# A two-layer diffusion trunk on one core: layer 0's experts scatter four at a time per stream

## The chip, the cores and the metric

The kernel is one program on one core of a Trainium2 chip. It is measured in microseconds of device time, from several runs, of which the median counts. TensorE does the matrix products, VectorE, ScalarE and POOL (GpSimd) the rest, and SyncE issues nearly all DMA transfers.

## What is computed

A trunk of two layers works on two streams of 256 tokens with 1024 channels: the context (stream 0) and the latents (stream 1). Each layer mixes tokens by three branches (an S5 state-space scan, latent attention, window attention) and then applies a mixture of sixteen experts. Layer 0 does it for both streams, layer 1 for the latents alone. The part that matters here is the mixture:

```python
def expert_choice_ffn(h, lp):
    B, N, D = h.shape
    cap = CAPACITY_FACTOR * N // N_EXPERTS
    aff = jax.nn.softmax((h @ lp['w_router']).astype(jnp.float32), axis=-1)
    g, idx = lax.top_k(aff.swapaxes(1, 2), cap)
    xs = jax.vmap(lambda hb, ib: hb[ib])(h, idx)
    a = jnp.einsum('becd,edf->becf', xs, lp['w_gate'])
    u = jnp.einsum('becd,edf->becf', xs, lp['w_up'])
    y = jnp.einsum('becf,efd->becd', jax.nn.silu(a) * u, lp['w_down']) * g[..., None].astype(h.dtype)
    return jax.vmap(lambda ib, yb: jnp.zeros((N, D), yb.dtype).at[ib.reshape(-1)].add(yb.reshape(-1, D)))(idx, y)
```

Every expert picks its 32 best tokens of each stream, transforms them, weights them with the router's affinity and adds them back at the places of those tokens. The last line is the scatter.

## The kernel before

The network is written in Python with a framework that schedules: instructions are recorded in the order of the code, and a scheduler then sets the order in which they stand on each engine, by its own model of times. On each engine the order is fixed once the program is built; an instruction that waits holds up what stands behind it there.

**Weights.** `expert_ring` (L1391) is the stream of expert weights: tiles of 1 MB, twelve an expert (four each of gate, up and down), 192 a layer. Each tile has a buffer of 2048 columns, taken from a list `ready`; when TensorE has used up a tile its buffer goes back to the list and the next load is issued on SyncE's queue (`load`, L229). Every buffer carries the index of the load from which on it is no longer used for weights. In layer 0 some 21 buffers serve at first; five of them (the blocks big0 to big2) end with load 100, because layer 1's S5 set-up needs them, four with 160 and two with 172. Five are left at the end: the four halves of h0 and h1 and one piece of the arena.

**One expert.** `moe` (L1565) loops over the experts e. In layer 0 the two streams stand together: M = 64 rows (stream, slot), and the 1024 output columns are cut in CT = 2 pieces of NF = 512, which stand below each other on the 128 partitions of one PSUM tile. Gate and up products go to two PSUM tiles `sc`; ScalarE takes tanh (L1613), VectorE makes the gated product (L1614, L1615); four transposes (`tp`, L246) turn it and ScalarE copies it out (L238); the down product goes to a PSUM tile `mm`. All these products are recorded under L243, the helper `mm`. The tokens of experts 4g to 4g + 3 are collected by `gather` (L1544), again products into the PSUM tiles `F` and `ad`, after experts 0, 3, 6 and 8.

**The scatter.** VectorE weights the down product with the sixth modulation row and puts it into YS (L1635). YS has 128 rows and is filled by GE = 2 experts: (expert, stream, slot). Then a selection matrix is built for each of the four token tiles t (two per stream): the rows (expert, slot) of that stream are compared with the tokens' slots and multiplied by half the affinity (L1644, L1645), the rows of the other stream stay zero from a memset (L1631). It is transposed into a `tp` tile and copied into CM. Each tile t takes two products of 128x512 with CM as the weights and YS as the moving data, into `F` and `ad`, and VectorE adds each to the residual x[t] (L1659). After the last expert the products are accumulated in PSUM on top of x[t], brought in by a product with the identity, in the tiles `F`, `ad`, `sc`, `sc`, `tp`, `tp`, `mm`, `mm`. In short:

```python
if e % GE == GE - 1:
    scat = lambda pt, n, h, start: self.mm(pt, CM[:, n * 128:(n + 1) * 128], YS[:, halves[h]], start, True)
    for n, t in enumerate(tts):
        for h, hs in enumerate(halves):
            pt = self.ps(("F", "ad")[h])
            scat(pt, n, h, True)
            v.tensor_tensor(x[t][:, hs], x[t][:, hs], pt, op=OP.add)
```

**Beside it.** From expert 8 on `moe` also runs `s5_setup` (L507) for layer 1, three steps an expert. It begins with parameters of 48 KB (`in_s5_prm`), two powers on POOL (L549, L551), a chain of small VectorE operations (L546 and others), and then transposes on TensorE into `tp` tiles, in four rounds.

Of the kernel before, what the change touches and what calls it, by code (L numbers as in the profile page):

```python
# [9 lines left out]
AF = mybir.ActivationFunctionType  # L10
# [4 lines left out]
D = 1024  # L15
# [16 lines left out]
# ---------------------------------------------------------------- shape-only constants  # L32
# [125 lines left out]
class Net:  # L158
# [6 lines left out]
    # ------------------------------------------------------------ helpers  # L165
# [6 lines left out]
    def rot(self, name, cols, n, low=False, at=None):  # L172
        """n buffers used in turn: returns a function that gives the next one"""
# [21 lines left out]
    # ------------------------------------------------------------ work that fills the gaps of the tensor engine  # L195
# [3 lines left out]
    def tick(self, us):  # L199
        """issue about us of the work that waits in the queue"""  # L200
# [57 lines left out]
    def pow_(self, out, in_, e):  # L258
        """out = in_ ** e"""
# [19 lines left out]
    def ln_apply(self, out, x, eng="v"):  # L279
        """out = (x - mean) * rstd"""  # L280
# [13 lines left out]
    def ln_affine(self, P, x, y, gb, again=True, eng="v"):  # L294
        """x = LN(P) g + b, P: halves of the columns; y: scratch; gives minus mean and 1 / deviation of x"""
# [34 lines left out]
    def ln_final(self, out, x, nm, r2):  # L330
        """out = (x + nm) r2"""
# [6 lines left out]
    # ------------------------------------------------------------ adaLN parameters  # L338
# [12 lines left out]
    def ada_group(self, l, g, bufs=None):  # L351
        """columns 2048 g .. of the adaLN parameters: mods 2g and 2g + 1"""
# [33 lines left out]
    def mod_row(self, l, m, s, dst, scale=1.0):  # L386
        """dst [128, 1024] = mod m of stream s on every partition"""
# [17 lines left out]
    def put(self, dst, src):  # L405
        """src into the parts dst [rows, 2, n]"""
# [9 lines left out]
    def block(self, tag, dtype):  # L416
        """a block that serves one purpose after another"""
# [3 lines left out]
    def branch_parts(self, l, b, oT, q0):  # L421
        """both parts of a branch output, [128, 4, 512 - q0]"""
# [17 lines left out]
    def wsplit(self, st, a, n, scale=None):  # L440
        """weights st [128, a, n] (times scale [128, a, n]) in two parts: a function of row k (and columns)"""
# [37 lines left out]
        # two blocks (row block, stream) at a time; of the second layer first those of the context  # L479
# [26 lines left out]
    # ------------------------------------------------------------ S5: matrices from the parameters  # L506
    def s5_setup(self, l, S, NP):  # L507
        """matrices of the layer from its parameters, NP group pairs at a time"""
# [72 lines left out]
        # powers a^1 .. a^4 (r: real, imaginary, minus real, minus imaginary)  # L581
# [16 lines left out]
        # phase of a^4 in turns, in [-1/2, 1/2]  # L598
# [19 lines left out]
        for j0 in range(0, 16, NP):  # L618
# [7 lines left out]
            # bb = q b  # L626
# [9 lines left out]
            # a^k bb and c a^k, state-major  # L636
# [25 lines left out]
            # chunk input matrices: (s, h) of a group on partitions, states on columns  # L662
# [1278 lines left out]
```

## Time and profile before

| what | us |
|---|---|
| median of 3 runs | 2170.84 |
| lowest and highest run | 2166.41, 2172.0 |
| span of the profiled execution | 2167.7 |
| TensorE busy in it | 1856.2 (86%) |
| VectorE busy | 1041.5 (48%) |
| ScalarE busy | 613.4 (28%) |
| POOL busy | 454.4 (21%) |

The profiled execution is one execution of its own. Its span runs from the first to the last instruction; no other time of it is given, so the sum is made against the span, which lies 3.1 us below the median. Busy time on TensorE is modelled, since products overlap: a row of several products says when the first starts and how long all of them take together. "x8" behind a product in float32 counts records, of which one product leaves two. A row of the timeline gives start, length, engine, line, operation, output and input, count, and in brackets the idle time before it with what ended it. DMA share is the mean busy share of the core's 16 DMA engines; values just above 1 mean they never rested.

### The profile page before, as it was taken

The page shows a single profiled execution, that of the slowest core. Times are in us where ns is not written, and L with a number is a line of the kernel's source. Part 1 is how long each engine was busy: PE and PEld are TensorE (multiplying, and loading weights), DVE is VectorE, ACT ScalarE, POOL GpSimd, SP SyncE. Part 2 cuts the span into 40 slices and gives each one's busy share as a digit, 9 for nine tenths or more (in the row PEclk, how much of TensorE's full clock was granted, in tenths as well). Part 3 has the DMA queues.
Part 4 walks back from the last instruction along what each step waited for, and adds up shares of the span by engine and source line. Part 5 has one row for each costly group of instructions (what it writes and reads, how often), then busy time and mean ns, then how long its engine had stood idle before and what let it go on. Part 6 is the DMA issues. An engine that isn't in the chain of part 4 may idle for free. (4 is left out here: it accounts for less than half of the span.)

```text
span 2167.7 us, 31197 instructions
## 1 busy us (share of the span) xinstructions
PE 1856.2 (86%) x12121; PEld 1117.8 (52%) x12121; DVE 1041.5 (48%) x2463; ACT 613.4 (28%) x1353; POOL 454.4 (21%) x592
## 2 busy tenths in 40 slices
PE   5998999999998799999798979889998766666665
PEld 2876666666776434343333358777786533222222
DVE  7767666644538512222555165978767311010102
ACT  2344343433434311010111054654553100000000
POOL 5735420000135100000434033642114000000000
PEclk8999999999999899999899989899999787686766
DMA  7234533265347799989899823242267799999996
GB/s 304 65 127 142 159 131 111 72 206 185 92 133 285 273 382 409 409 350 378 329 375 355 324 76 96 74 142 79 75 221 249 303 409 409 409 409 409 409 409 271
DMA packets 222163, 544.16 MB, mean 251 GB/s; under 512 B 18624, under 2 KB 101696, under 8 KB 221120
## 3 DMA queue, kind: packets, MB, share of 16 engines
q1 hardware_dynamic: 222016, 542.18, 67.6%
q8 instruction: 95, 1.56, 0.3%
q14 instruction: 52, 0.43, 0.1%
HBM read 541.09 MB, written 1.05 MB: 250 GB/s over the span
## 5 line engine op out<-in xcount | busy, mean ns | idle before, releaser
L243 PE MATMUL F<-h,wc 128*128 128x256 f32 (+1 forms) x1200 | 239.5, 351 | 13.9 <-ACT arena L1291 9.7
L400 ACT ACTIVATE wc<-arena 128x512 fp32r<-128x512 f32 (+2 forms) x280 | 170.2, 619 | 229.3 <-DMA arena<-in_w_in 49.4
L403 DVE TENSOR_TENSOR wc<-arena,wc 128x512 fp32r<-128x512 f32 (+2 forms) x205 | 163.8, 809 | 121.7 <-ACT wc L400 120.7
L243 PE MATMUL sc<-arena,xs 128*32 128x256 f32 (+1 forms) x1176 | 171.8, 535 | 56.7 <-DMA arena<-in_w_up 36.3
L243 PEld LDWEIGHTS F<-h,wc 128*128 128x128 f32 x1200 | 189.6, 197 | 47.9 <-ACT arena L1291 10.8
L246 PE MATMUL tp<-const,arena 128*128 128x128 f32 (+2 forms) x835 | 137.6, 291 | 62.8 <-DVE arena L1615 13.4
L403 POOL TENSOR_TENSOR wc<-arena,wc 128x512 fp32r<-128x512 f32 (+2 forms) x75 | 99.3, 1324 | 431.1 <-ACT wc L400 305.9
L243 PE MATMUL mm<-arena 128*32 128x256 f32 (+5 forms) x1076 | 168.1, 460 | 16.4 <-DMA arena<-in_w_down 8.0
L246 PEld LDWEIGHTS tp<-const,arena 128*128 128x128 f32 (+2 forms) x835 | 98.4, 146 | 120.8 <-issue 34.8
L1635 DVE TENSOR_TENSOR arena<-mm,arena 32x256 f32<-32x256 f32 (+1 forms) x96 | 48.9, 510 | 220.5 <-PE mm L243 208.7
L238 ACT ACTIVATE arena<-tp 128x512 f32<-128x512 f32 (+3 forms) x142 | 63.1, 474 | 311.9 <-PE tp L246 311.4
L260 POOL TENSOR_TENSOR lnq<-lnq,k 128x1 f32<-128x1 f32 x22 | 16.4, 747 | 574.5 <-DVE lnq L307 538.3
L243 PEld LDWEIGHTS sc<-arena,xs 128*32 128x32 f32 (+1 forms) x1176 | 54.4, 134 | 152.0 <-issue 81.9
L243 PE MATMUL sc<-h,xs 128*32 128x256 f32 (+1 forms) x760 | 118.7, 529 | 15.6 <-DMA h<-in_w_up 8.2
L1613 ACT ACTIVATE arena<-sc 128x512 f32<-128x512 f32 (+1 forms) x32 | 15.7, 490 | 366.3 <-PE sc L243 364.0
L243 PEld LDWEIGHTS mm<-arena 128*64 128x64 f32 (+2 forms) x1076 | 69.6, 137 | 91.5 <-issue 44.5
L243 PE MATMUL sc<-big,xs 128*32 128x256 f32 (+1 forms) x688 | 95.0, 522 | 15.5 <-DMA big<-in_w_gate 8.9
L1615 DVE TENSOR_TENSOR arena<-arena,sc 128x512 f32<-128x512 f32 (+1 forms) x32 | 17.7, 553 | 176.1 <-PE sc L243 175.7
L243 PE MATMUL mm<-wc,h 128*128 128x512 f32 (+2 forms) x288 | 78.4, 397 | 11.0 <-ACT h L492 6.1
L243 PE MATMUL F<-extra,wc 128*128 128x256 f32 (+1 forms) x432 | 85.0, 342 | 2.7 <-DVE arena L1326 2.4
L546 DVE TENSOR_TENSOR arena<-arena 128x64 f32<-128x64 f32 (+2 forms) x300 | 81.5, 318 | 10.7 <-POOL arena L549 4.7
L243 PEld LDWEIGHTS sc<-h,xs 128*32 128x32 f32 (+1 forms) x760 | 36.5, 132 | 86.8 <-issue 49.8
(345 smaller groups left out, 3246.6 us busy)
## 6 DMA issues: line engine op xcount, KB each, us to landing
arena<-in_w_gate SPq DMA_DIRECT2D x53, 1024.0 KB, 11.3
arena<-in_w_down SPq DMA_DIRECT2D x48, 1024.0 KB, 12.5
arena<-in_w_up SPq DMA_DIRECT2D x44, 1024.0 KB, 18.2
arena<-in_w_ada SPq DMA_DIRECT2D x82, 512.0 KB, 4.6
h<-in_w_down SPq DMA_DIRECT2D x41, 1024.0 KB, 10.3
h<-in_w_up SPq DMA_DIRECT2D x37, 1024.0 KB, 10.5
arena<-in_w_in SPq DMA_DIRECT2D x66, 512.0 KB, 3.8
big<-in_w_gate SPq DMA_DIRECT2D x30, 1024.0 KB, 15.1
```

Of the source, the lines that this page charges most:

```text
L238: self.nc.scalar.activation(out, in_, AF.Copy)
L243: return self.nc.tensor.matmul(out, lhsT, rhs, start=start, stop=stop, skip_group_check=True)
L246: self.nc.tensor.transpose(out, in_, self.c("idn")[:n, :n])
L260: self.nc.gpsimd.tensor_tensor(out, in_, e.to_broadcast(list(in_.shape)), op=OP.pow)
L400: nc.scalar.activation(hi, src, AF.Copy)
L403: eng.tensor_tensor(lo, src, hi.bitcast(F32), op=OP.subtract)
L546: tt = lambda o, a, b, op: v.tensor_tensor(o, a, b, op=op)
L1613: nc.scalar.activation(th, gu[0][:, :NF], AF.Tanh, scale=0.5)
L1615: v.tensor_tensor(th, th, gu[1][:, :NF], op=OP.mult)
L1635: v.tensor_tensor(YS[o:o + M, c * NF:(c + 1) * NF], yp[M * c:M * c + M, :NF], m5[M * c:M * c + M], op=OP.mult)
```

## The change

In layer 0 four experts of one stream are scattered together. There are now two tiles YS, one per stream, each with the rows (expert, slot) of four experts, so that all 128 rows hold data; the weighted eviction writes 32 rows at a time. After every fourth expert the two streams follow one another: each builds the selection matrices of its own two token tiles, 128 rows without zeros, in one matrix `w` of 256 columns, transposes them, copies them into one CM of 256 columns, and does its four products. The memset goes. In layer 1, with one stream, the code does what it did. The place of CM in the arena moves. (The full diff also drops comments; those hunks are left out.)

```diff
-        GE = 128 // M
-        io = self.c("iota")[:, None, :].to_broadcast([128, GE, 32])
+        io = self.c("iota")[:, None, :].to_broadcast([128, 4, 32])
...
             if e == 0:
-                YS, w, CM = [self.buf(k, c, True, self.T[k]) for k, c in (("ys", D), ("rwt", NF), ("cm", NF))]
-                nc.gpsimd.memset(w, 0.0)
-                wv = w.rearrange("p (t e s c) -> p t e s c", t=nt, e=GE, s=NS)
-            o = (e % GE) * M
-            for c in range(CT):
-                v.tensor_tensor(YS[o:o + M, c * NF:(c + 1) * NF], yp[M * c:M * c + M, :NF],
-                                m5[M * c:M * c + M], op=OP.mult)
-            if e % GE == GE - 1:
-                g = e // GE
+                YS = [self.buf(f"ys{n}", D, True, self.T["ys"] + D * n) for n in range(NS)]
+                w, CM = [self.buf(k, 256, True, self.T[k]) for k in ("rwt", "cm")]
+                wv = w.rearrange("p (i e s) -> p i e s", i=2, e=4)
+            o = e % 4 * 32
+            for n in range(NS):
+                for c in range(CT):
+                    r = M * c + 32 * n
+                    v.tensor_tensor(YS[n][o:o + 32, c * NF:(c + 1) * NF], yp[r:r + 32, :NF], m5[r:r + 32], op=OP.mult)
+            if e % 4 == 3:
+                g = e // 4
...
-                for n, t in enumerate(tts):
-                    o = wv[:, n, :, n // 2]
-                    v.tensor_tensor(o, self.cd[t][:, es, None].to_broadcast([128, GE, 32]), io, op=OP.is_equal)
-                    v.tensor_tensor(o, o, self.ah[t][:, es, None].to_broadcast([128, GE, 32]), op=OP.mult)
-                    self.tr(tp[:, n * 128:(n + 1) * 128], wv[:, n].rearrange("p e s c -> p (e s c)"))
-                self.copy(CM, tp[:, :nt * 128], "a")
+                for n in range(NS):
+                    two = tts[2 * n:2 * n + 2]
+                    tp = self.ps("tp")
+                    for i, t in enumerate(two):
+                        v.tensor_tensor(wv[:, i], self.cd[t][:, es, None].to_broadcast([128, 4, 32]), io, op=OP.is_equal)
+                        v.tensor_tensor(wv[:, i], wv[:, i], self.ah[t][:, es, None].to_broadcast([128, 4, 32]), op=OP.mult)
+                        self.tr(tp[:, i * 128:(i + 1) * 128], wv[:, i].rearrange("p e s -> p (e s)"))
+                    self.copy(CM, tp[:, 0:256], "a")
+                    scat = lambda pt, i, h, start: self.mm(pt, CM[:, i * 128:(i + 1) * 128], YS[n][:, halves[h]], start, True)
...
+                    if e < 15:
+                        for i, t in enumerate(two):
+                            for h, hs in enumerate(halves):
+                                pt = self.ps(("F", "ad")[h])
+                                scat(pt, i, h, True)
+                                v.tensor_tensor(x[t][:, hs], x[t][:, hs], pt, op=OP.add)
+                        continue
...
-                   oh=14592, lngb1=15104, m2=17152, mht=8192, eth=4096, eht=4608, m5=5120, rwt=5632, ys=6144, cm=7168,
+                   oh=14592, lngb1=15104, m2=17152, mht=8192, eth=4096, eht=4608, m5=5120, rwt=5632, ys=6144, cm=5888,
```

The scheduler moves other instructions with it. Three places of TensorE's order matter. The names are PSUM tiles and their sources; a row with x4 is four products.

The first place is TensorE between experts 9 and 10, where the transposes of layer 1's S5 set-up begin (`tp_7150` to `tp_7177` before, `tp_7059` to `tp_7086` now; `sc_7107`, `sc_7108` and `sc_7016`, `sc_7017` are expert 10's gate and up, `mm_6991` is expert 9's down). Before, from the last scatter products of expert 9's group on:

```order
L243 MATMUL F_7101<-arena 128x512
L243 MATMUL ad_7104<-arena 128x512
L243 MATMUL sc_7107<-arena,xs 64x512 x4
L243 MATMUL sc_7108<-arena,xs 64x512 x4
L243 MATMUL sc_7108<-extra_5498,xs 64x512 x4
L243 MATMUL sc_7108<-extra_5499,xs 64x512 x4
L243 MATMUL sc_7108<-h_5504,xs 64x512 x4
L246 MATMUL tp_7150<-const,arena 128x128 x4
L246 MATMUL tp_7159<-const,arena 128x128 x3
L246 MATMUL tp_7168<-const,arena 128x128 x4
L246 MATMUL tp_7159<-const,arena 128x128
L246 MATMUL tp_7177<-const,arena 128x128 x4
```

Now, from expert 9's transposes on:

```order
L246 MATMUL tp_6985<-const,arena 128x128 x4
L243 MATMUL mm_6991<-h_5504,arena 64x512 x8
L243 MATMUL mm_6991<-h_5505,arena 64x512 x8
L243 MATMUL sc_7016<-arena,xs 64x512 x4
L246 MATMUL tp_7059<-const,arena 128x128 x3
L243 MATMUL sc_7016<-arena,xs 64x512 x4
L246 MATMUL tp_7059<-const,arena 128x128
L246 MATMUL tp_7068<-const,arena 128x128 x3
L243 MATMUL sc_7016<-arena,xs 64x512 x8
L246 MATMUL tp_7068<-const,arena 128x128
L246 MATMUL tp_7077<-const,arena 128x128 x4
L243 MATMUL sc_7017<-arena,xs 64x512 x4
```

The scatter behind expert 9 is gone, and the first S5 transposes stand behind four of expert 10's products; before they stood behind all thirty-two.

The second place is TensorE behind expert 7's down product (`mm_6626` before, `mm_6565` now; `sc_6686`, `sc_6687` and `sc_6629`, `sc_6630` are expert 8's gate and up). Before:

```order
L243 MATMUL mm_6626<-extra_5499,arena 64x512 x4
L243 MATMUL mm_6626<-h_5504,arena 64x512 x8
L243 MATMUL sc_6686<-h_5505,xs 64x512 x8
L243 MATMUL sc_6686<-arena,xs 64x512 x4
L243 MATMUL F_6662<-arena 128x512
L243 MATMUL ad_6665<-arena 128x512
L243 MATMUL sc_6686<-arena,xs 64x512 x4
L243 MATMUL sc_6687<-arena,xs 64x512 x4
L243 MATMUL F_6668<-arena 128x512
L243 MATMUL sc_6687<-arena,xs 64x512 x4
L243 MATMUL ad_6671<-arena 128x512
```

Now:

```order
L243 MATMUL mm_6565<-h_5504,arena 64x512 x8
L243 MATMUL F_6597<-arena 128x512
L243 MATMUL ad_6600<-arena 128x512
L243 MATMUL F_6603<-arena 128x512
L243 MATMUL ad_6606<-arena 128x512
L243 MATMUL F_6617<-arena 128x512
L243 MATMUL ad_6620<-arena 128x512
L243 MATMUL sc_6629<-h_5505,xs 64x512 x4
L243 MATMUL sc_6630<-arena,xs 64x512 x8
L243 MATMUL F_6623<-arena 128x512
L243 MATMUL ad_6626<-arena 128x512
```

The eight scatter products of the group stood between expert 8's products; now six of them follow one another right behind the down product.

The third place is TensorE at the end of the stage, around the last scatter. Before, from the first scatter product on (`const` marks the products with the identity):

```order
L243 MATMUL F_8214<-arena 128x512
L243 MATMUL ad_8215<-arena 128x512
L243 MATMUL sc_8218<-arena 128x512
L243 MATMUL sc_8219<-arena 128x512
L243 MATMUL tp_8226<-arena,const 128x512
L243 MATMUL tp_8227<-arena,const 128x512
L243 MATMUL mm_8230<-arena,const 128x512
L243 MATMUL mm_8231<-arena,const 128x512
L243 MATMUL tp_8226<-arena 128x512
L243 MATMUL tp_8227<-arena 128x512
L243 MATMUL mm_8230<-arena 128x512
L243 MATMUL mm_8231<-arena 128x512
```

Now, from within expert 15's down product `mm_8064`:

```order
L243 MATMUL tp_8113<-arena,const 128x512
L243 MATMUL mm_8064<-h_5505,arena 64x512 x8
L243 MATMUL mm_8064<-arena 64x512 x4
L243 MATMUL F_8093<-arena 128x512
L243 MATMUL ad_8094<-arena 128x512
L243 MATMUL sc_8097<-arena 128x512
L243 MATMUL sc_8098<-arena 128x512
L243 MATMUL tp_8114<-arena,const 128x512
L243 MATMUL mm_8117<-arena,const 128x512
L243 MATMUL mm_8118<-arena,const 128x512
L243 MATMUL tp_8113<-arena 128x512
L243 MATMUL tp_8114<-arena 128x512
```

One identity product (`tp_8113`) has moved ahead of the down product; the scatter of the first two token tiles is followed by three identity products instead of four.

## Rows read from the trace of the kernel before

**Rows 1.** Windows of layer 0's expert stage: length, engines, clock, DMA share, GB/s
```profile
core 0: us, PE busy (x) PEld busy (x) DVE busy (x) ACT busy (x) POOL busy (x), PEclk, DMA share, GB/s
770.00:960.00 190.00, 188.03 (x830) 71.07 (x827) 44.70 (x99) 19.66 (x33) 0.00 (x0) 1.00 1.02 403
960.00:980.00 20.00, 18.90 (x95) 7.61 (x95) 4.64 (x17) 3.04 (x6) 0.00 (x0) 1.00 0.57 209
980.00:1070.00 90.00, 85.55 (x370) 31.97 (x366) 33.41 (x114) 11.51 (x26) 14.50 (x15) 1.00 1.00 388
1070.00:1090.00 20.00, 12.64 (x82) 6.70 (x84) 10.18 (x45) 2.98 (x12) 10.28 (x38) 0.66 0.50 176
1090.00:1170.00 80.00, 73.63 (x386) 25.61 (x382) 52.17 (x198) 12.47 (x50) 38.63 (x133) 1.00 1.02 393
1170.00:1230.00 60.00, 55.76 (x262) 22.44 (x264) 17.02 (x41) 5.13 (x15) 5.01 (x17) 1.00 0.83 298
1230.00:1252.00 22.00, 18.91 (x82) 5.76 (x80) 2.65 (x4) 2.83 (x5) 0.00 (x0) 1.00 0.97 389
770.00:1252.00 482.00, 453.42 (x2096) 171.16 (x2094) 164.77 (x516) 57.63 (x146) 68.42 (x200) 0.99 0.95 367
```

**Rows 2.** Waits of SyncE's DMA queue, 760 to 1260 us: total, times, longest
```profile
SPq L229 <- PE sc L243: 237.9, 112, 7.0
SPq L229 <- PE mm L243: 128.4, 55, 13.5
```

**Rows 3.** Groups by form, 770 to 1266 us: count, busy, mean ns, idle before
```profile
L243 PE MATMUL sc<-h,xs 128*64 128x512 f32 x310 | 78.5, 600 | 4.1 <-DVE arena L1614 1.4 <-DMA h<-in_w_up 1.4 <-DMA h<-in_w_gate 1.3
...
L243 PE MATMUL F<-arena 128*128 128x512 f32 x58 | 31.7, 628 | 4.3 <-DVE arena L1635 4.3
...
L246 PE MATMUL tp<-const,arena 128*128 128x128 f32 x160 | 25.8, 299 | 17.0 <-DVE arena L546 9.0 <-DVE arena L1615 5.8 <-ACT big L238 2.0
...
L1635 DVE TENSOR_TENSOR arena<-mm,arena 64x512 f32<-64x512 f32 x32 | 22.0, 688 | 93.4 <-PE mm L243 82.4 <-PE sc L243 10.7
...
L1659 DVE TENSOR_TENSOR arena<-arena,F 128x512 f32<-128x512 f32 x28 | 19.2, 687 | 46.1 <-PE F L243 46.1
...
L238 ACT ACTIVATE arena<-tp 128x512 f32<-128x512 f32 x24 | 13.6, 596 | 92.8 <-PE tp L246 92.6
```

**Rows 4.** Timeline of PE at expert 5's scatter
```profile
917.44 1.10 PE L243 MATMUL F<-arena 128*128 128x512 f32 x2 [0.88 <-DVE arena L1635]
918.37 1.02 PE L243 MATMUL ad<-arena 128*128 128x512 f32 x2
919.32 1.12 PE L243 MATMUL F<-arena 128*128 128x512 f32 x2
```

**Rows 5.** Timeline of SyncE: issue of expert weights, two in a row
```profile
956.41 5.93 SPq L229 DMA_DIRECT2D arena<-in_w_up  x3
975.94 0.37 SPq L229 DMA_DIRECT2D extra<-in_w_up  x1
```

**Rows 6.** Timeline of PE before layer 1's first S5 transposes
```profile
1065.64 1.89 PE L243 MATMUL sc<-h,xs 128*64 128x512 f32 x8
1073.77 1.09 PE L246 MATMUL tp<-const,arena 128*128 128x128 f32 x4 [6.24 <-DVE arena L546]
```

**Rows 7.** Timeline of POOL: the two powers of that set-up
```profile
1029.46 5.43 POOL L549 TENSOR_TENSOR arena<-k,arena 128x32 f32<-128x32 f32 x1 [260.12 <-DMA arena<-in_s_prm]
1055.92 5.42 POOL L551 TENSOR_TENSOR arena<-k,arena 128x32 f32<-128x32 f32 x1 [21.03 <-DMA arena<-in_w_down]
```

**Rows 8.** Timeline of PE at the end of the stage
```profile
1254.47 1.10 PE L243 MATMUL F<-arena 128*128 128x512 f32 x2 [0.88 <-DVE arena L1635]
1256.27 1.88 PE L243 MATMUL sc<-arena 128*128 128x512 f32 x4
1257.98 1.88 PE L243 MATMUL tp<-arena,const 128*128 128x512 f32 x4
```

**Rows 9.** Windows, layer 1's expert stage (columns as in rows 1)
```profile
1740.00:2148.00 408.00, 270.17 (x2712) 104.84 (x2712) 48.54 (x116) 15.56 (x40) 0.00 (x0) 0.74 1.02 407
```

More of the change, by code (lines that the diff above doesn't have):

```diff
@@ L1629, in moe @@
             if e == 0:
-                YS, w, CM = [self.buf(k, c, True, self.T[k]) for k, c in (("ys", D), ("rwt", NF), ("cm", NF))]
-                nc.gpsimd.memset(w, 0.0)
-                wv = w.rearrange("p (t e s c) -> p t e s c", t=nt, e=GE, s=NS)
-            o = (e % GE) * M
-            for c in range(CT):
-                v.tensor_tensor(YS[o:o + M, c * NF:(c + 1) * NF], yp[M * c:M * c + M, :NF],
-                                m5[M * c:M * c + M], op=OP.mult)
-            if e % GE == GE - 1:
-                g = e // GE
-                es = slice(GE * g, GE * g + GE)
-                tp = self.ps("tp")
-                for n, t in enumerate(tts):
-                    o = wv[:, n, :, n // 2]
-                    v.tensor_tensor(o, self.cd[t][:, es, None].to_broadcast([128, GE, 32]), io, op=OP.is_equal)
-                    v.tensor_tensor(o, o, self.ah[t][:, es, None].to_broadcast([128, GE, 32]), op=OP.mult)
-                    self.tr(tp[:, n * 128:(n + 1) * 128], wv[:, n].rearrange("p e s c -> p (e s c)"))
-                self.copy(CM, tp[:, :nt * 128], "a")
-                halves = [slice(0, 512), slice(512, 1024)]
-                scat = lambda pt, n, h, start: self.mm(pt, CM[:, n * 128:(n + 1) * 128], YS[:, halves[h]], start, True)
-                if g == 0:
-                    for t in tts:
-                        x[t] = self.buf(f"x{t}", D, True, D * ((t + 2) % 4))
-                        nc.scalar.activation(x[t], xn[t], AF.Identity, bias=self.back[t][:, 1:2], scale=self.back[t][:, 0:1])
-                if e < 15:
-                    for n, t in enumerate(tts):
-                        for h, hs in enumerate(halves):
-                            pt = self.ps(("F", "ad")[h])
-                            scat(pt, n, h, True)
-                            v.tensor_tensor(x[t][:, hs], x[t][:, hs], pt, op=OP.add)
-                else:
-                    pts = {}
-                    for n0 in range(0, nt, 2):
-                        for n in (n0, n0 + 1):
-                            t = tts[n]
-                            pts[t] = [self.ps(tag) for tag in (("F", "ad"), ("sc", "sc"), ("tp", "tp"), ("mm", "mm"))[n]]
-                            for h, hs in enumerate(halves):
-                                i = self.mm(pts[t][h], self.c("idn"), x[t][:, hs], True, False)
-                                if n0:
-                                    tc.keep_in_program_order(i)
-                        for n in (n0, n0 + 1):
-                            for h in range(2):
-                                tc.keep_in_program_order(scat(pts[tts[n]][h], n, h, False))
@@ L1673, in moe @@
-        self.free("m5", "rwt", "cm", "ys", "eth", "eht", "slots")
+                YS = [self.buf(f"ys{n}", D, True, self.T["ys"] + D * n) for n in range(NS)]
[6 more added lines that the diff above has]
+                    v.tensor_tensor(YS[n][o:o + 32, c * NF:(c + 1) * NF], yp[r:r + 32, :NF], m5[r:r + 32], op=OP.mult)
@@ new lines, in moe @@
+            if e % 4 == 3:
+                g = e // 4
+                es = slice(4 * g, 4 * g + 4)
+                halves = [slice(0, 512), slice(512, 1024)]
+                pts = {}
+                for n in range(NS):
[7 more added lines that the diff above has]
+                    scat = lambda pt, i, h, start: self.mm(pt, CM[:, i * 128:(i + 1) * 128], YS[n][:, halves[h]], start, True)
+                    if g == 0:
+                        for t in two:
+                            x[t] = self.buf(f"x{t}", D, True, D * ((t + 2) % 4))
+                            nc.scalar.activation(x[t], xn[t], AF.Identity, bias=self.back[t][:, 1:2], scale=self.back[t][:, 0:1])
+                    if e < 15:
[5 more added lines that the diff above has]
+                        continue
+                    for i, t in enumerate(two):
+                        pts[t] = [self.ps(tag) for tag in (("F", "ad"), ("sc", "sc"), ("tp", "tp"), ("mm", "mm"))[2 * n + i]]
+                        for h, hs in enumerate(halves):
+                            j = self.mm(pts[t][h], self.c("idn"), x[t][:, hs], True, False)
+                            if n:
+                                tc.keep_in_program_order(j)
+                    for i, t in enumerate(two):
+                        for h in range(2):
+                            tc.keep_in_program_order(scat(pts[t][h], i, h, False))
@@ L1674, in moe @@
+        self.free("m5", "rwt", "cm", *[f"ys{n}" for n in range(NS)], "eth", "eht", "slots")
         return pts
```

## The prediction, made before the changed kernel ran

> **What bounds the stage now.** I read the stage windows first. Layer 0's sixteen experts take from 770 to 1252 us, and over them TensorE is busy 453 of 482 us at a granted clock of 0.99, while the DMA engines have a share of 0.95 [rows 1]. Both look full, so busy time alone does not say who waits; the waits do. SyncE's queue, which issues every expert weight, stood 238 + 128 = 366 us waiting for TensorE to finish with a weight tile [rows 2]. TensorE in turn hardly waited for weights: the gate and up products from the h blocks stood idle 4.1 us in the whole stage, 2.7 of them for a load [rows 3]. So TensorE is the pace, with DMA close behind it: at its full rate of about 403 GB/s and a share of 1.02 in most windows, and visibly idle in three, 960 to 980 (0.57), 1070 to 1090 (0.50) and 1170 to 1230 (0.83) [rows 1]. Measured against 1.02, that is 8.8 + 10.2 + 11.2 = **30 us of idle DMA**. This is the room: however fast TensorE becomes, the weights still have to arrive.
>
> The three gaps have visible causes. In the first, SyncE issues nothing between 962 and 976 us [rows 5], because five tiles of the ring are given up there to the set-up of layer 1's S5. In the second, TensorE stands 6.24 us before the first transposes of that set-up [rows 6]. The third lies where the ring is down to seven and then five tiles and expert 13's scatter runs between the products.
>
> **The change, part by part.**
>
> *Scatter products removed.* Before, eight groups of eight products; now four groups of eight. The products that go are those after experts 1, 5, 9 and 13. Consecutive ones start 0.93 to 0.95 us apart [rows 4], so 32 x 0.95 = **30.4 us** less on TensorE. The half of zero rows made none of them shorter: what now has 128 useful rows costs the same.
>
> *Waits in front of them.* The first scatter of a group waits 0.88 us for VectorE's eviction [rows 4]; the F products waited 4.3 us for it over the stage, five times [rows 3]. Three of these go: **2.5 us**.
>
> *Selection transposes.* 16 of 32 go. At 299 ns of record each that is at most 4.8 us [rows 3], at least nothing: behind the transposes of the expert's own activations they filled the time in which ScalarE copies those out (596 ns, [rows 3]). I take 0.
>
> *VectorE.* The weighted eviction becomes four 32-row operations an expert instead of two of 64 rows: 32 more. No row here is 32x512; the nearest are 64x512 at 688 ns, the same columns [rows 3], and I take that value, 22 us more. The 32 accumulations that go take 687 ns each [rows 3], 22 us less. Sum zero, and none of it bounds TensorE except where an accumulation is queued behind four evictions. That happens after expert 7: the new order puts F, ad, F, ad, F, ad in a row. The second F needs the first accumulation, which now stands behind four evictions, 4 x 0.69 = 2.8 us, against two products of 0.95 and the first wait of 0.88: about 0.7 us lost. The third F also needs stream 1's copy into CM, which cannot start until stream 0's four products have read CM: at most 0.6 us (half of a 596 ns copy, plus hand-overs). **1.4 us** lost there, between 0 and 3.
>
> *The two streams share CM.* After experts 3 and 11 other products stand between the streams and hide the copy. At the very end they do not: the third identity product into the tp banks waits for that copy. Against this, one identity product (0.95 us) has moved ahead of the last down product. I take 0 for the tail [rows 8], between -1 and +2.
>
> *S5 set-up of layer 1.* Its transposes now stand after only four of expert 10's products instead of all thirty-two, so TensorE arrives early. The chain they wait for is two powers on POOL of 5.4 us each [rows 7], the small VectorE operations behind them, 12.4 us from the end of the second power (1061.34) to the first transpose (1073.77) [rows 6, 7]. The first power started when its 48 KB had landed, and the second stood 21 us behind it because VectorE's one multiplication between them was queued behind scatter accumulations [rows 7]. Those are gone, and the multiplication now stands right behind expert 9's gate, before its down product instead of after it. Counted in products, chain and TensorE meet with a stall like that of today, six to seven us. I charge **2 us**, between 0 and the 8.5 that expert 9's removed group gives.
>
> *Memset.* One 128x512 memset on POOL goes; POOL does nothing else in this part of the stage (busy 0.00 from 770 to 980 [rows 1]), so nothing.
>
> Sum on TensorE: 30.4 + 2.5 - 1.4 - 2 = **29.5 us**, just under the 30 us that the DMA engines have to spare. They will not use all of it: with five tiles in the ring at the end, an issue still waits for a product. I leave 2.5 us of idle DMA, and forecast **27 us**. Layer 1 follows with nothing but a shift: its order differs in a few products of one attention stage only, and its expert stage is bound by loads (share 1.02, [rows 9]) that start from layer 1's own work. The profiled execution spans 2167.7 us, 3.1 below the median of the runs, 2170.8; the same difference on the median gives **2144 us**.
>
> **Rivals.**
>
> *The loads are the bound already.* By this one the gaps at 960 and 1070 belong to the ring and the S5 set-up and stay whatever TensorE does; only the third gap can be filled, and there expert 13's group is worth 8 x 0.95 + 0.8 = 8.4 us: 2162. For it: share 1.02 for 190 us on end [rows 1]. Against it: SyncE's 366 us of waiting for TensorE [rows 2]. If TensorE is 16 us earlier by expert 7, releases run ahead of the loads by that much, and the 14 us without an issue [rows 5] are covered by a queue that is still draining.
> The Trainium skill speaks for this rival (Perfetto Trace Analysis, Identifying the Most-Contended Engine): matmul busy time is a bad measure, since matmuls are pipelined, and 94% of busy TensorE would prove little. By that rule the sum would be the rival's 8 us. Here the waits, not the busy time, carry the argument.
>
> *The S5 chain takes all of expert 9's gain.* The stall before the transposes grows from 6 to 14 us and 8.5 us go: 27 - 8.5 = 18.5 gained, 2152. It decides if VectorE's chain starts no earlier than today.
>
> *Slower: TensorE's clock falls in the last experts.* With less work TensorE has holes, as in layer 1's expert stage, where it is busy 270 of 408 us and the granted clock is 0.74 [rows 9]. A weight tile costs eight records, 1.89 us at 2.4 GHz [rows 6]; an expert's twelve tiles take 22.7 us, at 1.2 GHz 45, and with some 5 us of transposes and gathers 50, against a pace of 482 / 16 = 30 us. Over the last four experts that costs 4 x 20 = 80 us, and 80 - 27 gives 2224. It decides when the busy share nears layer 1's 66%; taking 30 us off leaves (453 - 30) / (482 - 27) = 93%. Unlikely.
> The Trainium skill has the rule (TensorE: Matmul & The Clock Gate, HAM oscillation): gaps in which TensorE waits for DMA throw its clock back to half, and by it this rival's 2224 would come. The one window of the stage with a long stall agrees, 0.66 [rows 1]; nothing else here does.
>
> That the change does not do what it says is excluded by the order: 32 scatter products fewer, nothing added.
>
> **How the numbers follow.** Forecast case (gain 20 to 33): 0.68. S5 chain: 0.12. Loads the bound: 0.14. Clock: 0.03. An unseen reordering cost that eats it all: 0.03. 0.3% is 6.5 us, about what a measurement of this kernel can tell from no change. The loads case at 2162 lies mostly beyond it, I give a third of it to no change with part of the last case: faster 0.89, same 0.06, slower 0.05. The range goes from a gain of 35 us (the three gaps counted by GB/s instead of share: 20 x (1 - 209/403) + 20 x (1 - 176/403) + 60 x (1 - 298/403) = 36) to one of 9, which takes in the rival of the loads: **2136 to 2162**; the likeliest case alone would be 2138 to 2151.
>
> **What would show it.** F and ad products of 128x512 in layer 0 from 58 records each to 26 in the same stage; SyncE's gap at 962 to 976 gone or short; windows of the stage with a share above 1.0 up to the last experts; waits of TensorE for loads larger than today, since the slack is spent; a stall of 5 to 9 us before the S5 transposes. I would be wrong if the gaps stayed with the same length, or if the granted clock fell under 0.9 after 1090 us.

## The result, and the profile after

The changed kernel takes **2136.66 us** (median of 4 runs, 2133.11 to 2137.85) beside 2170.28 us for the kernel before on the same chip: ratio 0.9846, 95% interval 0.9832 to 0.986. The gain is 33.6 us where 27 were forecast; the time lies just inside the range, at its fast end. The profiled execution spans 2134.4 us, 33.3 less than before.

All of it comes from layer 0's expert stage. The last down product of expert 15 ended at 1253.6 us, now at 1220.3; from there to the end both kernels take 914.1 us. The last records of that product, before and now:

```profile
1251.65 1.94 PE L243 MATMUL mm<-arena 128*64 128x512 f32 x8 [0.22 <-DMA arena<-in_w_down]
```
```profile
1218.40 1.89 PE L243 MATMUL mm<-arena 128*64 128x512 f32 x8
```

The stage windows of the changed kernel, columns as in [rows 1]:

```profile
770.00:960.00 190.00, 186.25 (x884) 72.81 (x883) 49.80 (x100) 21.95 (x39) 0.00 (x0) 1.00 1.02 399
960.00:980.00 20.00, 18.65 (x74) 6.68 (x73) 6.35 (x10) 1.23 (x3) 0.00 (x0) 1.00 1.03 409
980.00:1070.00 90.00, 76.38 (x414) 30.11 (x415) 47.91 (x196) 17.10 (x53) 37.15 (x93) 0.96 1.03 401
1070.00:1090.00 20.00, 17.26 (x96) 6.02 (x94) 10.19 (x46) 2.76 (x9) 7.47 (x26) 1.00 1.03 400
1090.00:1140.00 50.00, 44.29 (x206) 14.52 (x204) 31.55 (x102) 6.18 (x24) 24.10 (x82) 0.99 1.03 404
1140.00:1170.00 30.00, 28.19 (x161) 11.08 (x158) 7.82 (x19) 3.45 (x12) 0.53 (x1) 0.97 0.95 351
1170.00:1200.00 30.00, 26.59 (x120) 10.83 (x121) 4.32 (x7) 1.79 (x3) 0.00 (x0) 1.00 0.99 378
1200.00:1220.00 20.00, 18.42 (x78) 5.63 (x76) 3.27 (x8) 2.03 (x4) 0.00 (x0) 1.00 0.88 348
800.00:1140.00 340.00, 312.83 (x1524) 119.40 (x1522) 139.14 (x437) 41.96 (x118) 68.72 (x199) 0.99 1.03 406
770.00:1220.00 450.00, 416.02 (x2018) 157.69 (x2017) 161.20 (x484) 56.49 (x146) 69.25 (x200) 0.99 1.01 394
```

The gap at 960 to 980 is closed (0.57 to 1.03), the one at 1070 to 1090 too (0.50 to 1.03), and from 800 to 1140 us the DMA engines do not rest. Behind 1140 us they still do, at a share of 0.95, 0.99 and 0.88. The last row sums it up: the stage moves what it moved before (177.05 MB then, 177.13 MB now, by the DMA view) at 394 GB/s instead of 367 [rows 1], in 450 us instead of 482.

The waits of SyncE's queue on TensorE, 760 to 1227 us (total, times, longest), beside the 237.9 and 128.4 us of [rows 2]:

```profile
SPq L229 <- PE sc L243: 155.6, 83, 10.5
SPq L229 <- PE mm L243: 74.9, 36, 6.3
```

And SyncE's timeline over the place of [rows 5], where nothing was issued for 14 us:

```profile
961.23 6.86 SPq L229 DMA_DIRECT2D h<-in_w_down  x3
969.43 2.40 SPq L229 DMA_DIRECT2D arena<-in_w_gate  x1
```

An issue there now takes about 2.3 us, where the lone one of [rows 5] took 0.37. All 166 issues of expert weights in the stage windows took 63.5 us before and take 226.2 now, while the two waits for TensorE fell from 366 to 230 us. So the issuer now spends more of its time in the issues themselves; a queue that is full with loads would explain it, but no row names the cause. The groups by form, 770 to 1233 us, that answer to [rows 3]:

```profile
L243 PE MATMUL sc<-h,xs 128*64 128x512 f32 x312 | 76.6, 609 | 8.0 <-DVE arena L1613 4.0 <-DMA h<-in_w_up 2.0 <-DMA h<-in_w_gate 2.0
...
L1637 DVE TENSOR_TENSOR arena<-mm,arena 32x512 f32<-32x512 f32 x64 | 44.0, 687 | 88.6 <-PE mm L243 87.6
...
L246 PE MATMUL tp<-const,arena 128*128 128x128 f32 x144 | 23.6, 288 | 15.1 <-DVE arena L546 7.6 <-DVE arena L1614 6.2 <-ACT big L238 1.0
...
L243 PE MATMUL F<-arena 128*128 128x512 f32 x26 | 14.4, 636 | 3.2 <-DVE arena L1637 1.9 <-DVE arena L1662 0.8 <-ACT arena L238 0.5
```

The records of F went from 58 to 26 (those of ad too), a 32x512 eviction takes 687 ns as the 64x512 did, and TensorE waits a little more for loads.

### The profile page after: what moved, and what is told of

It is laid out like the page before. It is cut to its first block, busy times and chain, and to the rows that moved or that the text cites. A ratio compares the mean times of both kernels' runs of the same rounds, so it can differ in the third digit from the quotient of the medians.

```text
span 2134.4 us, 30999 instructions
## 1 busy us (share of the span) xinstructions
PE 1818.9 (85%) x12041; PEld 1107.7 (52%) x12041; DVE 1042.8 (49%) x2431; ACT 612.2 (29%) x1353; POOL 452.3 (21%) x590
## 5 line engine op out<-in xcount | busy, mean ns | idle before, releaser
L243 PE MATMUL sc<-arena,xs 128*32 128x256 f32 (+1 forms) x1176 | 167.1, 528 | 54.2 <-DMA arena<-in_w_up 31.5
L1637 DVE TENSOR_TENSOR arena<-mm,arena 32x512 f32<-32x512 f32 (+1 forms) x128 | 70.9, 554 | 215.6 <-PE mm L243 213.9
L243 PE MATMUL sc<-h,xs 128*32 128x256 f32 (+1 forms) x760 | 114.1, 520 | 22.1 <-DMA h<-in_w_up 10.4
L1613 DVE SCALAR_TENSOR_TENSOR arena<-arena,sc 128x512 f32<-128x512 f32 (+1 forms) x32 | 17.8, 555 | 165.4 <-ACT arena L1612 165.4
L243 PE MATMUL mm<-wc,h 128*128 128x512 f32 (+2 forms) x288 | 78.7, 398 | 11.7 <-ACT h L492 6.8
## 6 DMA issues: line engine op xcount, KB each, us to landing
h<-in_w_up SPq DMA_DIRECT2D x37, 1024.0 KB, 15.8
```

Source lines behind the costliest of these rows:

```text
L243: return self.nc.tensor.matmul(out, lhsT, rhs, start=start, stop=stop, skip_group_check=True)
L1613: v.scalar_tensor_tensor(th, th, 1.0, gu[0][:, :NF], op0=OP.add, op1=OP.mult)
L1637: v.tensor_tensor(YS[n][o:o + 32, c * NF:(c + 1) * NF], yp[r:r + 32, :NF], m5[r:r + 32], op=OP.mult)
```

## Experiments

All times are medians; the kernel before ran beside each group, at 2168.7 to 2170.9 us, so a difference between two groups is uncertain by some 2 us.

### Give TensorE its products back

Sixteen products, or thirty-two with `range(2)` for i:

```diff
+            if full and e in (1, 5, 9, 13):
+                for n in range(2):
+                    for i in range(1):
+                        for h in range(2):
+                            pt = self.ps(("F", "ad")[h])
+                            self.mm(pt, self.c("idn")[0:64], YS[n][0:64, 512 * h:512 * h + 512], True, True)
```

> The changed kernel with 16 extra 128x512 products (a 64-row piece of the identity times the rows of YS, into F and ad, read by nobody) behind experts 1, 5, 9 and 13 of layer 0, one token tile per stream. No VectorE addition, selection transpose or copy is added. Theory (the 32 products taken off TensorE are the gain): 16 products of 0.95 us come back, 15 us, and some of them stand inside gate and up pairs: 12 to 18 us slower than the changed kernel, 2149 to 2155 us. Rival (in the changed kernel the loads set the pace and TensorE has room): 0 to 4 us slower, 2137 to 2141 us. In between, about 2143, if the room on the DMA side and TensorE's time are both nearly used up.

> As the run with 16 extra products, with both token tiles of each stream: 32 extra 128x512 products, as many as the change removed, and still without the VectorE additions, selection transposes and copies. Theory (TensorE's products are the whole of the gain): 28 to 34 us slower than the changed kernel, 2165 to 2171 us, the time before. Rival (the loads set the pace): under 8 us, up to 2145 us. Second rival (half of the gain was VectorE's additions or the waits for evictions): 15 to 20 us slower, 2152 to 2157 us.

Measured: 2150.65 us (ratio to before 0.9918, 0.9891 to 0.9945) and 2158.05 (0.995, 0.9934 to 0.9965), so 14.0 and 21.4 us above the changed kernel. The first sixteen cost 0.87 us each, nearly what a scatter product takes; the loads did not hide them. (The extra products sum over 64 rows where a scatter product sums over 128. They are no shorter for it: the 32 took 30.8 us from one record's start to the next, 0.96 each.) Thirty-two give back 21 of the 33 us, less than the theory's 28 and more than either rival. Two windows of the run with 32 show where it differs from the kernel before:

```profile
960.00:980.00 20.00, 18.68 (x92) 6.81 (x90) 4.86 (x16) 1.97 (x5) 0.00 (x0) 1.00 0.67 259
...
1060.00:1090.00 30.00, 24.81 (x152) 9.54 (x149) 19.56 (x83) 4.63 (x19) 14.54 (x52) 1.00 1.02 384
```

The first gap is back (0.67, before 0.57), the second is not: the share at 1060 to 1090 is 1.02 at a clock of 1.00, where the kernel before had 0.50 and 0.66 in 1070 to 1090 [rows 1]. So part of the 12 us that are missing hangs on that place and not on the number of products; the runs with a moved S5 set-up look into it.

### Take more products away

The first kernel is the changed one, the second the kernel before:

```diff
+                    if full and e < 15:
+                        continue
                     if e < 15:
                         for i, t in enumerate(two):
```
```diff
-                if e < 15:
+                if full and e in (1, 5, 9, 13):
+                    pass
+                elif e < 15:
```

> The changed kernel without layer 0's scatter products and additions behind experts 3, 7 and 11 (24 products of 128x512 and 24 additions; the contribution of the first twelve experts to layer 0's output is left out, the selection transposes stay). Theory (the changed kernel stands at the DMA bound with 5 us of idle DMA left in the experts' stage): 2 to 6 us faster than the changed kernel, 2131 to 2135 us. Rival (TensorE still sets the pace by itself): 24 x 0.95 = 23 us faster, 2114 us. In between, near 2125, if the loads' own rate rises further than the share shows.

> The kernel before without the products and additions behind experts 1, 5, 9 and 13 (32 products and 32 additions; these experts' and their partners' part of layer 0's output is left out; the selection transposes and the copies of the groups stay). Theory (the number of products is the whole of it, the new layout of rows and the joining of four experts do nothing): 30 to 36 us faster than the kernel before, 2134 to 2140 us, like the changed kernel. Rival (the later and joined scatter, or the rows' new places, gave a good part of the gain): under 25 us faster, above 2145 us.

Measured: 2135.33 us (0.984, 0.9815 to 0.9866) and 2130.37 (0.9823, 0.9801 to 0.9845). Twenty-four products fewer than in the changed kernel, 23 us of TensorE, bring 1.3 us on the median, just under the 2 to 6 expected (its four runs spread from 2130.4 to 2139.8). With the runs above this is a kink right at the changed kernel: more products cost nearly their full time, fewer gain nearly nothing. TensorE's waits (us, times, longest) in the kernel without them, 780 to 1222 us, show the time come back as waits for loads, among others:

```profile
PE sc L243 <- DVE arena L1613: 9.8, 3, 5.6
PE sc L243 <- DMA h<-in_w_up: 8.8, 7, 3.4
...
PE sc L243 <- DMA arena<-in_w_gate: 5.6, 8, 1.1
PE sc L243 <- DMA h<-in_w_gate: 5.3, 5, 2.8
```

The same three loads cost 2.0 us each in the changed kernel. The second run gains all that the change gained, with the old layout of rows: 39.3 us, 3 more than its theory allowed; its interval overlaps the change's. What counts is that 32 products are gone, and joining four experts is how that is done without losing their output.

### Fewer bytes

```diff
-                i = self.load(ap, self.ins[nm][l, e].rearrange("(k p) (c n) -> p k c n", p=128, n=NF)[:, kh:kh + 2])
+                nk = 1 if l == 0 and 3 <= e <= 10 and r == 5 else 2
+                i = self.load(ap[:, 0:nk], self.ins[nm][l, e].rearrange("(k p) (c n) -> p k c n", p=128, n=NF)[:, kh:kh + nk])
```

> The kernel without the scatter products behind experts 3, 7 and 11 (2135 us, 24 products fewer than the changed kernel, and 1 to 6 us faster than it), and with half of one w_up tile left unloaded in each of the experts 3 to 10 (8 pieces of 512 KB; these products use what the tile held before). Theory (with that much room on TensorE the stage takes as long as its bytes take at 400 GB/s): 8 x 0.524 MB / 0.400 MB per us = 10.5 us less, 8 to 11 us faster than without the products alone, 2124 to 2127 us. Rival (not the loads, but TensorE's other work, the evictions or the S5 set-up stop the kernel there): 0 to 3 us faster, 2132 to 2135 us.

Measured: 2122.9 us (0.9786, 0.9768 to 0.9804), 12.4 below the run without the products on the medians and 6.8 by the profiled spans (2121.8 beside 2128.6); the intervals do not overlap. The theory's 8 to 11 lies between the two. 2.4% fewer of the stage's bytes (4.19 of 177 MB) gave what twenty-four products could not. So in that run, past the kink, the loads are the bound.

### The rest of a group: additions and selection work

The first kernel is the one before; the second adds to the run with 32 products the selection code of four more groups (comparisons, multiplications, transposes, copies into CM).

```diff
-                            v.tensor_tensor(x[t][:, hs], x[t][:, hs], pt, op=OP.add)
+                            if not full or e not in (1, 5, 9, 13):
+                                v.tensor_tensor(x[t][:, hs], x[t][:, hs], pt, op=OP.add)
```

> The kernel before with all its scatter products, but without the 32 VectorE additions into x behind experts 1, 5, 9 and 13 of layer 0 (the contribution of those experts and their partners to layer 0's output is left out). Theory (TensorE's products are what the change took off the path): 0 to 5 us faster than the kernel before, 2165 to 2170 us, and that only where an eviction follows its addition later than it could. Rival (the additions on VectorE, in the way of the evictions that TensorE waits for, were the last 12 us of the gain that the run with 32 extra products did not give back): 10 to 14 us faster, 2156 to 2160 us.

> The run with 32 extra products, and with it the selection work of those groups again: 16 transposes of 128x128, 16 comparisons and 16 multiplications on VectorE and 8 copies of 128x256 on ScalarE, read by nobody. Only the 32 additions of the kernel before are not there. Theory (the selection work costs TensorE its transposes, about 0.2 us each as the rows of before and after differ by 3.4 us, and little else): 2 to 5 us slower than with the products alone, 2160 to 2163 us. Rival (it stood beside idle time and cost nothing, as the prediction took it): 0 to 1 us, 2158 us. Second rival (it is the whole rest of the gain): 10 to 13 us, 2168 to 2171 us.

Measured: 2168.33 us (0.9996, 0.9986 to 1.0007), so 32 additions are worth nothing; and 2183.45 (1.0063, 1.0041 to 1.0086), 25 us above the run with the products alone, more than any theory gave. The rows of TensorE at layer 1's first S5 transposes in that run, and the windows there:

```profile
1064.82 1.89 PE L243 MATMUL sc<-h,xs 128*64 128x512 f32 x8
1078.41 1.08 PE L246 MATMUL tp<-const,arena 128*128 128x128 f32 x4 [11.70 <-DVE arena L546]
...
1084.81 2.96 PE L243 MATMUL sc<-arena,xs 128*64 128x512 f32 x8
```
```profile
1070.00:1080.00 10.00, 1.08 (x4) 0.71 (x4) 9.79 (x56) 1.03 (x4) 7.00 (x25) 0.50 0.51 197
1080.00:1090.00 10.00, 7.53 (x44) 3.88 (x44) 4.93 (x21) 2.82 (x11) 7.16 (x25) 0.65 0.15 22
```

TensorE stands 11.7 us for VectorE's chain, the granted clock drops to 0.50, which is the lower level of 1.2 GHz, and the DMA engines fall to 22 GB/s. No product with a weight tile ran from 1066.7 to 1084.8 us, so no tile came free. Something else stood in the way as well: SyncE's queue also carries the S5 parameters, and their load `in_s_c`, next in line, waited for VectorE and POOL until 1087.5 us. This trace does not separate the two. In the run without the selection work the stall there was 2.28 us and the clock stayed at 1.00.

### Move the S5 set-up

The same line in the kernel before (late_b), in the changed kernel (late_a) and in the run with products and selection work (late_t):

```diff
-            elif e > 8 and nxt is not None:
+            elif e > 8 and e != 10 and nxt is not None:
```

> The kernel before, with no step of layer 1's S5 set-up in expert 10, so that its first transposes come an expert later and the set-up ends in expert 15 instead of 14. Theory (in the kernel before TensorE's stall of 9.0 us for the set-up, and the fall of the clock behind it, are on the path, since the loads have room): the stall in front of the set-up's first transposes is under 2 us, the clock stays at 1.00 there, and the kernel is 6 to 12 us faster than before, 2157 to 2163 us. Rival (the stall only moves, or the steps that now crowd experts 11 to 15 cost the same): within 3 us of before, 2166 to 2172 us.

> The changed kernel with the same delay of the S5 set-up. Theory (in the changed kernel the loads never stop while TensorE waits, so this stall of 7.1 us costs nothing): 0 to 3 us faster than the changed kernel, 2133 to 2137 us, with larger waits of TensorE for loads in place of the stall. Rival (the stall is on the path here as well): 6 to 12 us faster, 2125 to 2131 us.

> The run with 32 extra products and the selection work (2183 us), with the same delay of the S5 set-up. Theory (the selection work's 25 us were a stall of 11.7 us for the set-up, the fall of the clock to 0.50 and the gap that the loads had there; the selection work itself costs its transposes): 15 to 22 us faster than without the delay, 2161 to 2168 us. Rival (the selection work costs TensorE, VectorE or ScalarE these 25 us all along the stage): under 6 us faster, above 2177 us.

Measured: late_b 2164.49 us (0.9966, 0.9951 to 0.9981), 6.4 faster than before; late_a 2134.01 (0.9845, 0.9818 to 0.9872), no different from the changed kernel; late_t 2172.77 (1.001, 0.9994 to 1.0025), 10.7 faster than without the delay, where 15 to 22 were expected.

late_b met its time (6 to 12) but only half of its signs. The wait in front of the set-up's transposes is 0.90 us; yet a wait of 4.20 us for VectorE's gated product stands just ahead of it, and the clock, expected at 1.00, still falls:

```profile
1070.00:1080.00 10.00, 8.44 (x34) 3.62 (x36) 7.98 (x37) 1.07 (x4) 6.70 (x25) 0.69 0.65 253
```

So 6.4 us is what moving the set-up gave, with part of the gap still there. TensorE's waits in late_a, 780 to 1223 us:

```profile
PE sc L243 <- DMA h<-in_w_up: 6.5, 6, 2.0
...
PE sc L243 <- DMA arena<-in_w_gate: 5.7, 8, 1.4
```

and its windows:

```profile
1040.00:1130.00 90.00, 80.00 (x436) 27.45 (x434) 55.45 (x196) 15.35 (x61) 38.33 (x131) 1.00 1.03 401
1130.00:1200.00 70.00, 56.94 (x275) 19.38 (x272) 19.00 (x47) 5.24 (x15) 8.99 (x29) 0.95 1.03 408
```

The stall is gone from the list, waits for loads stand in its place, and the share is 1.03 up to 1200 us. The same stall costs about 6 us where TensorE sets the pace and nothing where the loads do. Of the change's 33.6 us, 21.4 come back with the products and 6.4 are what the moved set-up gave in the kernel before; the 6 that remain have no run of their own. The traces show where the time lies that the products did not give back: between expert 0's and expert 15's down products the run with 32 takes 12.2 us less than the kernel before, of which 5.2 are waits (4.9 of them for the S5 chain), 4.6 gate and up products and 3.4 selection transposes. In late_t the rest was not settled: a stall of 2.8 us and a DMA share of 0.33 at 1160 to 1170 stand later in it, so a part of the selection work's price seems only to have moved.

### Does a product between the halves of a pair cost more?

Gate and up products come in pairs: one writes the upper, one the lower 64 rows of a tile, and in a run of them eight records take 1.77 us. In the trace of after, gate and up took less than before (below), and this was to say why. The split kernel has `c == 0` where the other has `c == 1`:

```diff
+                        if full and e in (3, 7, 11) and k == kh:
+                            if c == 1:
+                                tc.keep_in_program_order(j)
+                            if c == 0:
+                                pt = self.ps(("F", "ad")[r % 2])
+                                tc.keep_in_program_order(self.mm(pt, self.c("idn")[0:64], YS[r // 2 % 2][0:64, 0:512], True, True))
```

> The changed kernel with 24 extra 128x512 products (64 rows of the identity times 64 rows of YS, unread), 8 in the gate and up products of each of the experts 3, 7 and 11 of layer 0, each pinned between the two halves of a pair that write the lower and the upper 64 rows of one tile. Theory (the two halves run side by side only when they follow each other at once, and a product between them costs 0.3 to 0.6 us beside its own 0.95): 8 to 14 us slower than the run with the same products behind whole pairs, about 2163 to 2170 us. Rival (a product costs its own time wherever it stands): within 2 us of that run, 2154 to 2160 us.

> The same 24 extra products in the same experts, each pinned behind the second half of its pair. By the two runs with 16 and 32 extra products (0.85 and 0.65 us for each), both theories say 16 to 22 us slower than the changed kernel, 2153 to 2159 us; the run is there to be compared with the one that splits the pairs.

Measured: 2171.15 us (1.0017, 1.0006 to 1.0028) and 2174.05 (1.002, 1.0006 to 1.0035). The theory falls: no difference. But both lie some 35 us above the changed kernel for 24 products, 1.5 us each, where the expectation was 16 to 22. Part of it is the stall at the S5 transposes again, 8.2 us in both. Another part stands in the gate and up products. From start to start the 24 products take 25.3 us (split) and 26.6 (whole), and all gate and up products 11.8 and 10.0 us more than in the changed kernel. Their largest group was 87.5 us there and is, split and whole:

```profile
L243 PE MATMUL sc<-arena,xs 128*64 128x512 f32 x352 | 95.6, 601 | 0.2 <-DMA arena<-in_w_up 0.2
```
```profile
L243 PE MATMUL sc<-arena,xs 128*64 128x512 f32 x352 | 91.4, 605 | 0.2 <-DMA arena<-in_w_up 0.2
```

In the timeline of the split run single products stand so between them:

```profile
883.81 1.12 PE L243 MATMUL F<-arena 128*128 128x512 f32 x2
884.87 1.07 PE L243 MATMUL sc<-big,xs 128*64 128x512 f32 x2
885.87 1.13 PE L243 MATMUL ad<-arena 128*128 128x512 f32 x2
```

A product (two records) alone takes 1.0 us, and in a run of eight records 0.44. A half that lost its partner seems to pair with the next one when one follows, which would explain why the place made no difference; that was only argued. What one interruption costs stays open.

## Why the prediction was right, and where its size was off

**TensorE the pace, the loads close behind: right,** and closer than thought. Sixteen products more cost 14 us, twenty-four fewer gain 1.3.

**32 x 0.95 = 30.4 us: right.** From one record's start to the next, F and ad products of 128x512 took 56.3 us between expert 0's and expert 15's down products, and now 25.1: 31.2 less.

**VectorE net zero: right.** The new eviction has the price taken (687 ns beside 688), and the additions are worth nothing.

**Expert 7's back-to-back products, 1.4 us: right.** In the changed kernel:

```profile
958.53 1.10 PE L243 MATMUL F<-arena 128*128 128x512 f32 x2 [0.88 <-DVE arena L1637]
...
961.31 1.12 PE L243 MATMUL F<-arena 128*128 128x512 f32 x2 [0.82 <-DVE arena L1662]
...
963.83 1.13 PE L243 MATMUL F<-arena 128*128 128x512 f32 x2 [0.53 <-ACT arena L238]
```

The first wait was there before; 0.82 for an addition behind four evictions and 0.53 for the copy into CM are new, 1.35 together. With them the waits in front of F went from 4.3 to 3.2, which is 2.5 - 1.4.

**Tail 0: right,** 914.1 us from the last down product on in both.

**Selection transposes 0: a little low.** By starts, the 128x128 transposes took 23.3 us and now 20.7. Not foreseen at all: the gate and up products took 6 us less (239.0 to 232.9 us of busy time in their four groups; 7.1 less from start to start), with fewer products between them: 42 unbroken stretches instead of 64. The two pinned runs, with 77 and 67 stretches, show the reverse.

**S5 set-up, a stall of 6 to 7 us, a charge of 2: right about the stall, wrong about its price.**

```profile
1032.00 0.87 PE L246 MATMUL tp<-const,arena 128*128 128x128 f32 x3 [7.11 <-DVE arena L546]
```

It stands there as forecast (before 6.24, [rows 6]), and the granted clock drops as well (0.96 in the window that holds it). But the loads run through it at 1.03, and late_a shows that it costs nothing any more. In the kernel before the same stall had opened the second gap of the DMA engines. SyncE's and TensorE's rows there:

```profile
1067.57 0.37 SPq L229 DMA_DIRECT2D h<-in_w_up  x1
1081.96 1.34 SPq L229 DMA_DIRECT2D arena<-in_s_c  x2
1085.88 0.37 SPq L229 DMA_DIRECT2D h<-in_w_up  x1
```
```profile
1083.72 5.55 PE L243 MATMUL mm<-h,arena 128*64 128x512 f32 x24
```

The S5 parameters `in_s_c` hold the queue until 1081.96, but the next weight load still waits 4 us more, for the first product with a weight tile since 1067.5.

**29.5 us on TensorE, 30 us of idle DMA, 2.5 left: the sizes that failed.** The forecast took the smaller of the two sums, less 2.5, and a gain of 33.6 exceeds both.

On TensorE, between expert 0's and expert 15's down products, the records took 435.7 us from start to start and now take 395.4: 40.3 less, where 30.4 were forecast. The scatter is 31.2 of it, the selection transposes 2.6, the gate and up products 7.1; the rest are small shifts (1.7 of them a gather that moved ahead of this stretch, which is no gain). Against this the waits rose by 5.3 us, from 29.5 to 34.8, where the sum had 0.9 more. 40.3 - 1.7 - 5.3 is the 33.3 us by which the span fell.

On the DMA side I summed 1.02 minus the share over three windows and took all others as full. The share was the wrong measure for the third: 0.83 of 1.02 is 81%, but 298 of 403 GB/s is 74%, so that window alone had 15.6 us of room instead of 11.2. The others were not quite full: 980 to 1070 had a share of 1.00 at 388 GB/s, and the changed kernel moves 401 there. The count by GB/s that I kept for the end of the range (36) was nearer. At the 406 GB/s that the changed kernel holds from 800 to 1140 us, the stage's 177.05 MB take 436 of the 482 us, 46 us of room; 33 of them were used, and most of the rest lies behind 1140 us (360 GB/s to 1220).

That the time still lies in the range, by 0.7 us, is owed to that end of the range; the likeliest case, from 2138 us on, missed it by 1.3.

The Trainium skill says to judge DMA by the memory's rate and not by the occupancy of its sixteen engines (Perfetto Trace Analysis, Identifying the Most-Contended Engine), and here the trace agrees: the share misjudged the third window, and four windows of the changed kernel at 1.03, from 960 to 1140 us, move 400 to 409 GB/s. Its table puts 100% at 358 GB/s for a core, and adds that a core alone can pull more, to about 120% (Engine Utilization); the trace agrees with that too, with 367 GB/s in the kernel before, 394 now and windows at 409, which is 114%.

**The rivals.** *Loads already the bound (2162)* fell: the gaps at 960 and 1070 closed. It came true one step later, for the changed kernel itself. *S5 takes expert 9's gain* fell with the stall at 7.1 us. *Clock falls* fell: 0.96 to 1.00 from 980 to 1200 us, although TensorE is busy only 416 of 450 us. (Layer 1's 66%, against which I held this rival, is the one other case I had; no run here shows at what share the clock falls.) The Trainium skill's rule on clock oscillation (TensorE: Matmul & The Clock Gate, HAM oscillation), which speaks of waits for DMA, did not come true as a lasting state in this stage. Single stalls bear it out, though for VectorE: 0.50 after 11.7 us of standing in one run.

## What to carry to other kernels

Count room on the DMA side by bytes over the best sustained rate, for the whole stage, not by idle share in the windows that look idle, and take it as an upper bound (46 us here, of which 33 were reached). Count what a change does to the products around those it removes (7 us here). When TensorE and the loads are within a few per cent of each other, test both sides of the kink: add work to one engine, take it away, and take bytes away; a stall is worth fixing only on the side that binds (6 us before, nothing after). A scatter product with half of its rows zero took as long as a full one (0.95 us), so pack the rows first.

## What was not expected of the hardware

Where the loads bind, many of SyncE's issues take 2.3 us instead of 0.37, and a 1 MB load of `in_w_gate` into the arena lands after a median of 15.8 us instead of 9.7. The rate is up to 409 GB/s meanwhile, which speaks for a full queue and against slower memory; no run separates the two. A wait of TensorE goes with starved loads, through the buffers it does not free: 176 GB/s from 1070 to 1090 us in the kernel before [rows 1], behind a stall of 6.24 [rows 6]. And a 64-row product of two records took 1.0 us alone and 0.44 in a run.
